# Dividing by the softmax sum after the V product, and chunk outputs inside the recurrence, in a two-layer RWKV-7/MLA decoder trunk

## The chip, the cores and the metric

The kernel runs on one core of a Trainium2 chip, as one program. The metric is the device time of one execution in microseconds (us), median of several runs. All times below are of this chip.

## What is computed

Two layers of a decoder trunk on 512 tokens, D = 1024, in float32, then a final RMSNorm. Each layer has a mixer and a gated MLP with a short convolution. The mixer runs two token mixers side by side on projections of the same normalised input. The reference, cut to the parts that the change touches:

```python
def step(state, inp):                      # RWKV-7, 8 heads x 64, one token after the other
    r_t, w_t, k_t, v_t, a_t, b_t = inp
    sa = einsum('bhij,bhj->bhi', state, a_t)
    state = state * w_t[:, :, None, :] + sa[..., None] * b_t[:, :, None, :] + v_t[..., None] * k_t[:, :, None, :]
    return state, einsum('bhij,bhj->bhi', state, r_t)
...
mu = mean(y, -1); var = mean(square(y - mu), -1)          # a norm per token and head
y = (y - mu) * rsqrt(var + LNX_EPS) * lnx_w + lnx_b
y_a = (y + bonus) * gate @ W_oA
...
s = (q_nope . k_nope + q_rope . k_rope) * scale           # MLA attention, 8 heads, causal, blocks of 128 queries
p = softmax(where(key_pos <= q_pos, s, NEG_INF), axis=-1)
y_b = (p @ v) @ W_oB
...
h = h + (sigmoid(g_A) * y_a + sigmoid(g_B) * y_b) @ W_out
```

## The kernel before

Activations lie transposed: 128 channels on the partitions, 512 tokens along the free axis. Large products are done with three float32r matmuls (a high and a low part of each operand, `mm3`, lines 245 to 248). Weights come as units of eight 128x128 blocks through SyncE's queue (`produce`, line 205); each is cast to its high part by ScalarE (line 201) and its low part is formed by VectorE (line 202), with two buffers each.

A mixer has three stages. The first projects and prepares, for each pair of heads, the matrices of the RWKV-7 recurrence over eight chunks of 64 tokens (`AM`, `AR`, `BT`, values in `Z`). The second inverts the small triangular matrices in `AM` and makes the latent projections of the attention. The third, from line 770, holds the change. It does two things at a time:

- **The recurrence** (loop over `c` from line 910). For each chunk: the product of the state with `AR` (line 918), a sum on VectorE into `xs` (line 921), the product with `AM` (line 928), a copy into `Z` (line 930), the product with `BT` (line 937), and the new state `St` from it and `tmp`, which GpSimd makes (lines 943 and 944). Each step needs the one before it.
- **The attention** (a generator, line 777). First remaining projections, then values `Vt` for all heads, then for each pair of heads p = 0..3 and query block b = 0..3 one step t = 4p + b: `scores(p, b)` (two products into two `sc` banks; VectorE adds the causal mask and takes the row minimum, line 834; ScalarE takes the exponential with its row sum, line 837; VectorE takes the reciprocal of the sum, line 838; ScalarE scales the row, line 839). One step later `turned` transposes each head's block with TensorE into the one `pt` bank (line 846) and copies it out to `PT`, by VectorE where b is even and ScalarE where it is odd (line 848). Two steps later `values` multiplies with `Vt` into the bank `po` (line 857); after b = 3 `split` casts `po` into the operand of the output projection (lines 279 and 280). Between these lie the projections of the next pair of heads (`project`, extra products with `q` on line 818 and `K` on lines 806 and 807), and in the last pair the first products of the RWKV output projection (`ow`).

TensorE's order is as traced (`manual_schedule`). `filler(n)` takes n segments of the attention, from one `yield` to the next, and puts them into TensorE's order between the steps of the recurrence, so that TensorE has work while the other engines prepare the next step. Before the change the recurrence takes 37 segments: up to the end of step t = 3. The order on the other engines, and on SyncE's queue for transfers, is set by a planner when the kernel is built, by its own estimate of when each instruction is ready; an engine then works in that order.

After the recurrence come four `chunk_out` (lines 951 to 971: the outputs of two chunks each, from `AR`, `St`, `AM` and `Z` into the two banks of `xy`, and a copy by ScalarE back to `Z`), with two segments behind each; then the norms of all four (`group_norm`: sums, mean and square on VectorE and ScalarE, the power on GpSimd on line 984; `group_scale` on GpSimd, line 989); six segments; then `yop` for each pair of heads: four transposes of `Z` into a bank of `xy` (line 993), two loads into the two buffers of the tag `yl` (lines 995 and 997), a product-and-sum and a product on VectorE (lines 998 and 999), and a split. Two segments stand after each two `yop`. Then the rest of the attention runs without anything between, and the rest of the RWKV output projection (`wtile(yops)`) follows.

PSUM has eight banks in this stage: two `sc`, two `xy`, one `pt`, one `po`, two for accumulation. `qk` has eight buffers of 128x512, for `K` and `q` of two pairs of heads.

Of the kernel before, what the change touches and what calls it, by code (L numbers as in the profile page):

```python
# [158 lines left out]
def build(ctx, tc, x, pos, wst, vecd, constd, out):  # L159
# [265 lines left out]
    def mixer(l, ops, nrm, wks):  # L425
        with ExitStack() as mx:
# [343 lines left out]
            with pool(name=f"tb{l}", bufs=2) as tb:  # L770
                def MT(name, tag, bufs=3):
                    return tb.tile([128, 512], F32, name=name, tag=tag, bufs=bufs)
# [4 lines left out]
                def attention(yops, ow):  # L777
# [22 lines left out]
                    def project(p):  # L800
                        psk = acc()
                        mm3(psk, [w[:, 128 * p:128 * p + 128] for w in lk], kvop, True, True)
                        ks[p] = []
                        for hh in range(2):
                            K = MT("K", "qk", 8)
                            A.copy(K[0:64, :], psk[64 * hh:64 * hh + 64, :])
                            G.tensor_copy(K[64:128, :], kp[64:128, :])
                            ks[p].append(K)
                        yield
                        qs[p] = []  # L810
                        for hh in range(2):
                            psq = acc()
                            for j in range(2):
                                mm3(psq, W.get(), qops[j], j == 0, j == 1)
                                if j == 0:
                                    yield
                            q = MT("q", "qk", 8)
                            V.tensor_tensor(q, psq, rq, ALU.mult)  # L818
                            qs[p].append(q)
                            yield  # L820

                    Ps, PTs, po = {}, {}, {}

                    def scores(p, b):
                        n = 128 * (b + 1)
                        sps = [sc(), sc()]
                        for hh in range(2):
                            PE.matmul(sps[hh][:, 0:n], qs[p][hh][:, 128 * b:128 * b + 128], ks[p][hh][:, 0:n],  # L828
                                      start=True, stop=True)
                        Ps[p, b] = []  # L830
                        for hh in range(2):
                            P = MT("P", "P", 4)
                            mn = tb.tile([128, 4], F32, name="mn", bufs=6)
                            V.tensor_tensor_reduce(out=P[:, 0:n], in0=sps[hh][:, 0:n],  # L834
                                                   in1=cst[:, C_CAUS + 512 - n:C_CAUS + 512], scale=-ATT_SCALE,
                                                   scalar=1e30, op0=ALU.add, op1=ALU.min, accum_out=mn[:, 0:1])
                            A.activation(P[:, 0:n], P[:, 0:n], AF.Exp, bias=mn[:, 0:1], scale=-1.0, accum_out=mn[:, 1:2])  # L837
                            V.reciprocal(mn[:, 2:3], mn[:, 1:2])  # L838
                            A.activation(P[:, 0:n], P[:, 0:n], AF.Copy, scale=mn[:, 2:3])  # L839
                            Ps[p, b].append(P)  # L840
# [10 lines left out]
                    def values(p, b):  # L851
# [8 lines left out]
                        if b == 3:  # L860
                            oops.append(split(xp, po[p], None, "xb", 8))

                    yield from project(0)
                    steps = [(p, b) for p in range(4) for b in range(4)]
                    for t in range(18):
# [41 lines left out]


                St = [None]
                for c in range(8):  # L910
# [3 lines left out]
                    if c:  # L914
# [34 lines left out]


                def chunk_out(i):
                    xy = xyt()
                    for p in range(4):
                        for e, hh in ((0, 0), (1, 1), (0, 1), (1, 0)):
                            c = 2 * i + e
                            ur, vr = rows(e)
                            k0 = 64 * hh
                            if c:
                                PE.matmul(xy[vr:vr + 64, hh, 64 * p:64 * p + 64], AR[p][k0:k0 + 64, c, vr:vr + 64],
                                          St[c][k0:k0 + 64, p, :], start=p == 0, stop=False, tile_position=(k0, vr))  # L960
                    for hh in range(2):
                        for p in range(4):
                            for e in range(2):
                                c = 2 * i + e
                                ur, vr = rows(e)
                                hd = 2 * p + hh
                                PE.matmul(xy[vr:vr + 64, hh, 64 * p:64 * p + 64], AM[:, hd, c, vr:vr + 64],
                                          Z[:, i, e, 64 * hd:64 * hd + 64], start=c == 0 and p == 0, stop=p == 3,
                                          tile_position=(0, vr))
                    A.copy(Z[:, i, 0, :].rearrange("p (q h i) -> p q h i", h=2, i=64),  # L970
                           xy[:, :, 0:256].rearrange("p h (q i) -> p q h i", i=64))


                def group_norm(i):
                    Y = Z[:, i, 0, :].rearrange("p (h i) -> p h i", i=64)
                    s2 = Z[:, i, 1, :].rearrange("p (h i) -> p h i", i=64)
                    mu = tb.tile([128, 24], F32, name="mu", bufs=4)
                    V.tensor_reduce(mu[:, 0:8], Y, mybir.AxisListType.X, ALU.add)
                    V.tensor_scalar(mu[:, 0:8], mu[:, 0:8], 1.0 / 64, None, ALU.mult)
                    V.tensor_tensor(Y, Y, mu[:, 0:8, None].to_broadcast([128, 8, 64]), ALU.subtract)  # L980
                    A.activation(s2, Y, AF.Square)
                    V.tensor_reduce(mu[:, 8:16], s2, mybir.AxisListType.X, ALU.add)
                    V.tensor_scalar(mu[:, 8:16], mu[:, 8:16], 1.0 / 64, LNX_EPS, ALU.mult, ALU.add)
                    G.tensor_tensor(mu[:, 16:24], mu[:, 8:16], mhalf[:, 0:8], ALU.pow)  # L984
                    return mu[:, 16:24]

                def group_scale(i, gr):
                    Y = Z[:, i, 0, :].rearrange("p (h i) -> p h i", i=64)
                    G.tensor_tensor(Y, Y, gr[:, :, None].to_broadcast([128, 8, 64]), ALU.mult)  # L989

                def yop(ps, p):
# [177 lines left out]
```

## Time and profile before

| what | value |
|---|---|
| three runs | 1609.90, 1610.43, 1611.07 us |
| median | 1610.43 us |
| profiled execution | 1608.68 us |
| its span, from the first instruction to the last | 1606.9 us |
| share of TensorE in the chain of work that ended last | 90% |
| the same of VectorE, ScalarE, GpSimd | 5%, 2%, 2% |
| bytes moved | 166.08 MB, a mean of 103 GB/s |

The profile is of one execution. Its page and the views of its trace use short names: PE is TensorE's matmuls, PEld its weight loads, DVE is VectorE, ACT is ScalarE, POOL is GpSimd, SP is SyncE. L846 is line 846 of the kernel. An entry `out<-in` names the tiles written and read. A line of the view of waits reads "engine, tile, line that waited <- engine, tile, line that ended the wait: us in all, times, the longest". The granted clock is TensorE's: 1.00 is full speed. The chain is followed back from the last instruction, at each step to what released it. In a timeline the columns are start and duration in us, then engine, line, operation and shape, and in brackets the time that the engine stood idle ahead of it and what ended that.

### The profile page before, as it was taken

The page shows a single profiled execution, that of the slowest core. Times are in us where ns is not written, and L with a number is a line of the kernel's source. Part 1 is how long each engine was busy: PE and PEld are TensorE (multiplying, and loading weights), DVE is VectorE, ACT ScalarE, POOL GpSimd, SP SyncE. Part 2 cuts the span into 40 slices and gives each one's busy share as a digit, 9 for nine tenths or more (in the row PEclk, how much of TensorE's full clock was granted, in tenths as well). Part 3 has the DMA queues.
Part 4 walks back from the last instruction along what each step waited for, and adds up shares of the span by engine and source line. Part 5 has one row for each costly group of instructions (what it writes and reads, how often), then busy time and mean ns, then how long its engine had stood idle before and what let it go on. Part 6 is the DMA issues. An engine that isn't in the chain of part 4 may idle for free.

```text
span 1606.9 us, 22378 instructions
## 1 busy us (share of the span) xinstructions
PE 1559.8 (97%) x9052; PEld 1259.2 (78%) x9052; DVE 916.8 (57%) x1468; ACT 661.8 (41%) x996; POOL 188.7 (12%) x156
## 2 busy tenths in 40 slices
PE   8999999889999999999999999997999999999998
PEld 6887886668888888888878888765688888888887
DVE  6578786656555555533346768756465555554333
ACT  6445344563443333322244443455434433333222
POOL 1011002300211101100001111113003111110000
PEclk9999999899999999999999999999999999999999
DMA  6333321224422323233343223212243223233232
GB/s 209 112 102 128 121 85 63 78 63 140 132 92 94 103 92 100 97 105 123 116 136 112 95 97 117 87 61 79 66 152 124 92 92 105 92 95 102 92 101 83
DMA packets 57272, 166.08 MB, mean 103 GB/s; under 512 B 6352, under 2 KB 8528, under 8 KB 57168
## 3 DMA queue, kind: packets, MB, share of 16 engines
q1 hardware_dynamic: 57024, 164.48, 31.2%
q8 instruction: 71, 1.16, 0.3%
q14 instruction: 33, 0.27, 0.1%
q10 hardware_dynamic: 144, 0.16, 0.0%
HBM read 147.32 MB, written 17.30 MB: 102 GB/s over the span
## 4 chain that ended last, share of the span: by engine, by line
PE 90%; DVE 5%; ACT 2%; POOL 2%; issue 1%; DMA 1%; POOLq 0%; DVEq 0%; SPq 0%; ACTq 0%
PE acc L246 26%; PE acc L247 26%; PE acc L248 26%; PE sc L828 2%; PE xy L928 1%; PE pt L846 1%; PE m L599 1%; POOL mu L984 1%; PE po L857 1%; PE m L607 1%; ACT whi L201 1%; POOL Z L989 1%; DVE wlo L202 1%; ACT P L837 1%; ACT P L839 0%
## 5 line engine op out<-in xcount | busy, mean ns | idle before, releaser
L246 PE MATMUL acc<-hi,whi 128*128 128x512 f32 (+1 forms) x1910 | 755.1, 395 | 6.3 <-ACT hi L282 5.2
L248 PE MATMUL acc<-hi,wlo 128*128 128x512 f32 (+1 forms) x1910 | 742.1, 389 | 0.6 <-DVE wlo L202 0.6
L247 PE MATMUL acc<-lo,whi 128*128 128x512 f32 (+1 forms) x1910 | 741.1, 388 | 0.0
L201 ACT CAST whi<-raw 128x1024 fp32r<-128x1024 f32 (+2 forms) x249 | 253.4, 1019 | 546.9 <-PE acc L247 468.6
L246 PEld LDWEIGHTS acc<-hi,whi 128*128 128x128 f32 x1910 | 359.6, 188 | 82.8 <-ACT hi L282 5.2
L248 PEld LDWEIGHTS acc<-hi,wlo 128*128 128x128 f32 x1910 | 359.5, 188 | 75.8 <-DVE wlo L202 1.0
L247 PEld LDWEIGHTS acc<-lo,whi 128*128 128x128 f32 x1910 | 359.8, 188 | 72.3 <-DVE lo L283 0.5
L202 DVE TENSOR_TENSOR wlo<-raw,whi 128x1024 fp32r<-128x1024 f32 (+2 forms) x249 | 308.3, 1240 | 177.8 <-ACT whi L201 177.3
L1089 POOL TENSOR_TENSOR c<-c,rstd 128x512 f32<-128x512 f32 x44 | 58.0, 1317 | 403.5 <-ACT c L1088 403.5
L1082 DVE TENSOR_TENSOR u<-acc,rstd 128x512 f32<-128x512 f32 x44 | 30.4, 692 | 104.7 <-PE acc L248 104.6
L1091 DVE TENSOR_TENSOR c<-c,acc 128x512 f32<-128x512 f32 x44 | 30.3, 688 | 86.4 <-POOL c L1089 86.4
L1088 ACT ACTIVATE c<-c 128x512 f32<-128x512 f32 x44 | 27.8, 632 | 81.6 <-DVE c L1087 81.6
L837 ACT ACTIVATE P<-P,mn 128x128 f32<-128x128 f32 (+3 forms) x64 | 35.7, 558 | 57.4 <-DVE mn L834 57.0
L341 POOL TENSOR_TENSOR nacc<-nacc,nsq 128x512 f32<-128x512 f32 x14 | 25.1, 1790 | 245.4 <-ACT nsq L340 245.4
L305 POOL TENSOR_TENSOR nv<-nv,cst 128x4 f32<-128x4 f32 (+1 forms) x10 | 10.0, 996 | 352.1 <-DVE nv L304 352.1
L828 PE MATMUL sc<-K,q 128*128 128x128 f32 (+3 forms) x128 | 47.2, 494 | 1.3 <-DVE q L818 1.3
L834 DVE CUSTOM_DVE_ANT_0 P<-sc,cst 128x128 f32<-128x128 f32 (+3 forms) x64 | 30.5, 488 | 30.2 <-PE sc L828 29.5
L846 PE MATMUL pt<-cst,P 128*128 128x128 f32 x160 | 32.0, 301 | 15.5 <-ACT PT L848 11.5
L450 DVE TENSOR_TENSOR cur<-acc,rstd 128x512 f32<-128x512 f32 x28 | 19.1, 689 | 46.9 <-PE acc L248 39.3
L846 PEld LDWEIGHTS pt<-cst,P 128*128 128x128 f32 x160 | 20.6, 151 | 28.4 <-ACT PT L848 14.5
L1085 ACT ACTIVATE c<-u,vec 128x512 f32<-128x512 f32 x44 | 35.7, 811 | 2.8 <-DVE u L1081 2.8
L839 ACT ACTIVATE P<-P,mn 128x128 f32<-128x128 f32 (+3 forms) x64 | 33.2, 553 | 5.6 <-DVE mn L838 5.4
(242 smaller groups left out, 1374.9 us busy)
## 6 DMA issues: line engine op xcount, KB each, us to landing
raw<-in_w SPq DMA_DIRECT2D x238, 512.0 KB, 3.4
gate_d<-gg SPq DMA_DIRECT2D x32, 256.0 KB, 2.1
AM<-gate_d SPq DMA_DIRECT2D x16, 256.0 KB, 4.3
gb<-gate_d SPq DMA_DIRECT2D x16, 256.0 KB, 3.7
h<-in_x SPq DMA_DIRECT2D x8, 256.0 KB, 4.1
rgate_d<-gt SPq DMA_DIRECT2D x8, 256.0 KB, 2.7
bl_d<-rk SPq DMA_DIRECT2D x8, 256.0 KB, 2.0
bl<-bl_d SPq DMA_DIRECT2D x8, 256.0 KB, 2.6
```

The source lines that it names most:

```text
L201: A.copy(hi, r)
L202: V.tensor_tensor(lo, r, hi.bitcast(F32), ALU.subtract)
L246: PE.matmul(ps, w[0], xx[0], start=first, stop=False)
L247: PE.matmul(ps, w[0], xx[1], start=False, stop=False)
L248: PE.matmul(ps, w[1], xx[0], start=False, stop=last)
L828: PE.matmul(sps[hh][:, 0:n], qs[p][hh][:, 128 * b:128 * b + 128], ks[p][hh][:, 0:n], start=True, stop=True)
L834: V.tensor_tensor_reduce(out=P[:, 0:n], in0=sps[hh][:, 0:n], in1=cst[:, C_CAUS + 512 - n:C_CAUS + 512], scale=-ATT_SCALE, scalar=1e30, op0 ...
L837: A.activation(P[:, 0:n], P[:, 0:n], AF.Exp, bias=mn[:, 0:1], scale=-1.0, accum_out=mn[:, 1:2])
L839: A.activation(P[:, 0:n], P[:, 0:n], AF.Copy, scale=mn[:, 2:3])
L846: PE.transpose(pt[:, 128 * kb:128 * kb + 128], Ps[p, b][hh][:, 128 * kb:128 * kb + 128], ident)
L1085: A.activation(cc, u[:, 2:514], AF.Identity, bias=vc(l, "conv_b", i), scale=vc(l, "conv_w", 2 * FT + i))
L1089: G.tensor_tensor(cc, cc, rstd, ALU.mult)
```

## The change

Five things change together.

1. The exponentials of the attention are no longer scaled. The row sums of a pair of heads go into columns of one small tile `sums[p]`, and reciprocals and scalings per block go away. One step after the last block of a pair (`inverse`, t = 4p + 4) VectorE takes the eight reciprocals at once and GpSimd spreads them into a 128x512 tile `r`. At the end of the next step (`inverse_rows`, t = 4p + 5) TensorE transposes `r` in four blocks into the `pt` bank. The last values product of the pair (`values(p, 3)`) is put behind these transposes, where it was between the two `turned` of that step. Then ScalarE copies `po` to `o`, VectorE multiplies `o` with the `pt` bank, and `o` is split as `po` was.
2. `chunk_out` for the first three pairs of chunks moves into the recurrence, at c = 2, 4 and 6, in place of two segments each, and each is followed at once by its norm and scaling. It writes to two `sc` banks in place of `xy`, and ScalarE copies it out in two halves.
3. The recurrence thus takes 31 segments. After it come `chunk_out(3)`, its norm, and ten segments in place of six and of the two behind each `chunk_out`. `yop` is as it was.
4. `qk` has seven buffers in place of eight; there is a new tag `R` with two.
5. The size of the scratch for dynamic DMA is 512 in place of 1024.

The diff without the unchanged bodies of `group_norm` and `group_scale`, which only move up:

```diff
-                            K = MT("K", "qk", 8)
+                            K = MT("K", "qk", 7)
...
-                            q = MT("q", "qk", 8)
+                            q = MT("q", "qk", 7)
...
+                        if b == 0:
+                            sums[p] = tb.tile([128, 16], F32, name="ls", bufs=2)
                         for hh in range(2):
                             P = MT("P", "P", 4)
-                            mn = tb.tile([128, 4], F32, name="mn", bufs=6)
+                            mn = tb.tile([128, 1], F32, name="mn", bufs=6)
+                            j = 2 * b + hh
...
-                            A.activation(P[:, 0:n], P[:, 0:n], AF.Exp, bias=mn[:, 0:1], scale=-1.0, accum_out=mn[:, 1:2])
-                            V.reciprocal(mn[:, 2:3], mn[:, 1:2])
-                            A.activation(P[:, 0:n], P[:, 0:n], AF.Copy, scale=mn[:, 2:3])
+                            A.activation(P[:, 0:n], P[:, 0:n], AF.Exp, bias=mn[:, 0:1], scale=-1.0,
+                                         accum_out=sums[p][:, j:j + 1])
...
                         if b == 3:
-                            oops.append(split(xp, po[p], None, "xb", 8))
+                            o = MT("o", "R", 2)
+                            A.copy(o, po[p])
+                            V.tensor_tensor(o, o, inv[p], ALU.mult)
+                            oops.append(split(xp, o, None, "xb", 8))
+
+                    inv = {}
+
+                    def inverse(p):
+
+                        V.reciprocal(sums[p][:, 8:16], sums[p][:, 0:8])
+                        r = MT("r", "R", 2)
+                        G.tensor_copy(r.rearrange("p (j i) -> p j i", i=64), sums[p][:, 8:16, None].to_broadcast([128, 8, 64]))
+                        return r
+
+                    def inverse_rows(p, r):
+                        inv[p] = pb.tile([128, 512], F32, name="pt", tag="pt")
+                        for b in range(4):
+                            PE.transpose(inv[p][:, 128 * b:128 * b + 128], r[:, 128 * b:128 * b + 128], ident)
...
                             turned(*steps[t - 1], 0)
-                        if t > 1:
+                        if t > 1 and t % 4 != 1:
                             values(*steps[t - 2])
+                        elif t > 4:
+                            late = steps[t - 2]
                         if 0 < t < 17:
                             yield
                             turned(*steps[t - 1], 1)
+                        if t and t % 4 == 0:
+                            r = inverse(t // 4 - 1)
+                        if t > 1 and t % 4 == 1:
+                            inverse_rows(t // 4 - 1, r)
+                            values(*late)
                         yield
...
+                def chunk_out(i):
+                    ps = [sc("co"), sc("co")]
+                    begun = set()
+
+                    def put(e, hh, p, w, x, pos, last):
+                        ur, vr = rows(e)
+                        PE.matmul(ps[hh][vr:vr + 64, 64 * p:64 * p + 64], w, x, start=(e, hh) not in begun, stop=last,
+                                  tile_position=(pos, vr))
+                        begun.add((e, hh))
...
+                    for hh in range(2):
+                        A.copy(Z[:, i, 0, :].rearrange("p (q h i) -> p q h i", h=2, i=64)[:, :, hh, :],
+                               ps[hh][:, 0:256].rearrange("p (q i) -> p q i", i=64))
...
                         xs = xs.rearrange("p q h i -> p (q h) i")
-                        filler(2)
+                        if c in (2, 4, 6):
+                            chunk_out(c // 2 - 1)
+                            gr = group_norm(c // 2 - 1)
+                            group_scale(c // 2 - 1, gr)
+                        else:
+                            filler(2)
...
-                for i in range(4):
-                    chunk_out(i)
-                    filler(2)
-                grs = []
-                for i in range(4):
-                    grs.append(group_norm(i))
-                for i, gr in enumerate(grs):
-                    group_scale(i, gr)
-                filler(6)
+                chunk_out(3)
+                group_scale(3, group_norm(3))
+                filler(10)
...
-    nc = _bacc.Bacc("TRN2", target_bir_lowering=False, num_devices=1, dynamic_dma_scratch_size=1024)
+    nc = _bacc.Bacc("TRN2", target_bir_lowering=False, num_devices=1, dynamic_dma_scratch_size=512)
```

More of the change, by code (lines that the diff above doesn't have):

```diff
@@ L820, in project @@
                             yield
-                    Ps, PTs, po = {}, {}, {}
+                    Ps, PTs, po, sums = {}, {}, {}, {}
                     def scores(p, b):
@@ L906, in filler @@
                         next(att, None)
+                def chunk_out(i):
[6 more added lines that the diff above has]
+                        begun.add((e, hh))
+                    for p in range(4):
+                        for e, hh in ((0, 0), (1, 1), (0, 1), (1, 0)):
+                            c, k0 = 2 * i + e, 64 * hh
+                            vr = rows(e)[1]
+                            if c:
+                                put(e, hh, p, AR[p][k0:k0 + 64, c, vr:vr + 64], St[c][k0:k0 + 64, p, :], k0, False)
+                    for hh in range(2):
+                        for p in range(4):
+                            for e in range(2):
+                                vr = rows(e)[1]
+                                hd = 2 * p + hh
+                                put(e, hh, p, AM[:, hd, 2 * i + e, vr:vr + 64], Z[:, i, e, 64 * hd:64 * hd + 64], 0,
+                                    p == 3)
+                    for hh in range(2):
+                        A.copy(Z[:, i, 0, :].rearrange("p (q h i) -> p q h i", h=2, i=64)[:, :, hh, :],
+                               ps[hh][:, 0:256].rearrange("p (q i) -> p q i", i=64))
@@ new lines, in group_norm @@
+                def group_norm(i):
+                    Y = Z[:, i, 0, :].rearrange("p (h i) -> p h i", i=64)
+                    s2 = Z[:, i, 1, :].rearrange("p (h i) -> p h i", i=64)
+                    mu = tb.tile([128, 24], F32, name="mu", bufs=4)
+                    V.tensor_reduce(mu[:, 0:8], Y, mybir.AxisListType.X, ALU.add)
+                    V.tensor_scalar(mu[:, 0:8], mu[:, 0:8], 1.0 / 64, None, ALU.mult)
+                    V.tensor_tensor(Y, Y, mu[:, 0:8, None].to_broadcast([128, 8, 64]), ALU.subtract)
+                    A.activation(s2, Y, AF.Square)
+                    V.tensor_reduce(mu[:, 8:16], s2, mybir.AxisListType.X, ALU.add)
+                    V.tensor_scalar(mu[:, 8:16], mu[:, 8:16], 1.0 / 64, LNX_EPS, ALU.mult, ALU.add)
+                    G.tensor_tensor(mu[:, 16:24], mu[:, 8:16], mhalf[:, 0:8], ALU.pow)
+                    return mu[:, 16:24]
@@ L909, in mixer, with group_scale @@
+                def group_scale(i, gr):
+                    Y = Z[:, i, 0, :].rearrange("p (h i) -> p h i", i=64)
+                    G.tensor_tensor(Y, Y, gr[:, :, None].to_broadcast([128, 8, 64]), ALU.mult)
                 St = [None]
@@ L948, in mixer @@
                         filler(1)
[L951 to L971, printed above, removed]
@@ L974, in group_norm @@
[L974 to L985, printed above, removed]
@@ L987, in group_scale @@
-                def group_scale(i, gr):
-                    Y = Z[:, i, 0, :].rearrange("p (h i) -> p h i", i=64)
-                    G.tensor_tensor(Y, Y, gr[:, :, None].to_broadcast([128, 8, 64]), ALU.mult)
                 def yop(ps, p):
```

## The prediction

> **What bounds the kernel now.** I read the page first, for the share of each engine, then the table of stretches for the stage that the change touches, then the waits of TensorE in that stage, and the chain and the timelines only at the places that these waits name. In the page the first number of an engine is its busy time, the percentage its share of the span:
>
> ```profile
> PE 1559.8 (97%) x9052; PEld 1259.2 (78%) x9052; DVE 916.8 (57%) x1468; ACT 661.8 (41%) x996; POOL 188.7 (12%) x156
> ```
>
> TensorE is the bound, and its order is written out by hand. An instruction less on another engine is worth nothing unless TensorE waits for it. The change lies in the last stage of the mixer, once in each layer. The two rows give start and end, length, then the busy time of PE, PEld, DVE, ACT and POOL, the granted clock, and the DMA share:
>
> ```profile
> 232.00:365.00 133.00, 118.30 (x1120) 85.60 (x1115) 77.26 (x197) 69.65 (x155) 23.26 (x23) 0.94 0.23 73
> 1025.00:1160.00 135.00, 118.63 (x1153) 86.36 (x1154) 78.97 (x198) 69.99 (x156) 23.16 (x23) 0.96 0.23 73
> ```
>
> In 133 us TensorE stands idle for 14.7, in the second 135 for 16.4, and for some of the rest its clock is down. ACT and DVE are half idle: neither is a second bound. Who makes TensorE wait is in the view of waits, first layer 0, then layer 1 (total, times, longest):
>
> ```profile
> PE pt L846 <- ACT PT L848: 5.4, 3, 3.3
> PE xy L993 <- DVE bl L998: 4.7, 2, 3.8
> PE xy L993 <- POOL Z L989: 1.9, 1, 1.9
> PE pt L846 <- DVE PT L848: 1.7, 3, 0.9
> PE sc L828 <- DVE q L818: 0.7, 1, 0.7
> ```
>
> ```profile
> PE pt L846 <- ACT PT L848: 6.1, 4, 3.3
> PE xy L993 <- DVE bl L998: 4.7, 2, 3.8
> PE pt L846 <- DVE PT L848: 2.0, 4, 0.9
> PE xy L993 <- POOL Z L989: 1.9, 1, 1.9
> PE sc L828 <- DVE q L818: 0.7, 1, 0.7
> PE xy L993 <- DVE mn L838: 0.6, 1, 0.6
> ```
>
> That is 14.4 and 16.0 us. Each of the longest two waits is followed by a slow spell. The rows are two 4 us stretches of layer 0, one behind the wait of 3.8 and one behind that of 3.3, with a clock of 0.50; below them the chain shows the same scores (four records of 128x512) in a slow and in a full-speed place:
>
> ```profile
> 316.00:320.00 4.00, 4.00 (x15) 3.57 (x15) 1.73 (x8) 1.88 (x7) 0.00 (x0) 0.50 0.00 0
> 332.00:336.00 4.00, 3.74 (x6) 1.73 (x7) 1.10 (x3) 1.15 (x3) 0.00 (x0) 0.50 0.42 135
> ```
>
> ```profile
> 332.95 3.41 PE sc L828 x4
> ...
> 350.53 1.72 PE sc L828 x4
> ```
>
> So the question is which of these waits the change takes away, and which it makes. All terms below are per layer.
>
> **What it takes off other engines.** 32 normalisations on ACT and 32 reciprocals on DVE go; four copies, four products and four broadcast copies come. This is off the path, hidden under TensorE's work, except where a normalisation stands ahead of a copy that TensorE waits for. There is one such place, the wait of 3.3 at step t = 10. ACT's queue there:
>
> ```profile
> 328.17 1.05 ACT L201 CAST whi<-raw 128x1024 fp32r<-128x1024 f32 x1 [1.18 <-PE acc L247]
> ...
> 330.33 0.60 ACT L279 CAST hi<-bl 128x512 fp32r<-128x512 f32 x1
> 330.84 1.11 ACT L839 ACTIVATE P<-P,mn 128x384 f32<-128x384 f32 x2
> 331.86 0.35 ACT L848 COPY PT<-pt 128x256 f32<-128x256 f32 x1
> ```
>
> The copy of PT comes last, behind the cast of a weight unit, two exponentials, a cast of yop and two normalisations. Without these two it starts 1.0 earlier, 1.5 if the cast of yop has also moved away: I take 1.3 off and leave 2.0. The other two waits for ACT share 2.1; at t = 14 nothing but exponentials is left ahead of the copy, so I take 1.0 off there, and let 1.1 stand at t = 2. With a wait of 2.0 instead of 3.3 I take the slow spell behind it as gone: 1.7 from the scores (3.41 against 1.72) and 0.4 from the matmuls behind them, 2.1. If the clock falls all the same, that comes back.
>
> [...]
>
> **What it adds to TensorE.** The chain has four transposes of 128x128, one transpose alone, and a values call of four blocks:
>
> ```profile
> 341.62 0.59 PE pt L846 x4
> ...
> 344.47 0.11 PE pt L846
> 344.58 1.05 PE po L857 x16
> ```
>
> Sixteen transposes of r are 4 x 0.59 = 2.4, and nothing hides them: they are TensorE's own time.
>
> **The order around pt.** At t = 4p+5 the order was turned(0), values (1.05), turned(1); now it is turned(0), turned(1), four transposes into pt, then values. There is one pt bank. The values call was the cover of the copy out of it; now TensorE waits for that copy twice in a row. This is the copy on DVE:
>
> ```profile
> 272.88 0.29 DVE L848 COPY PT<-pt 128x128 f32<-128x128 f32 x1 [0.42 <-PE pt L846]
> ```
>
> A wait is at least about that 0.3; the longest wait for DVE above is 0.9, where another DVE pass stood ahead. I take 0.55, nearer to the bare copy, because DVE is half idle. Pairs 0 to 2 have two waits each (t = 17 has no turned): 6 x 0.55 = 3.3, between 1.8 and 5.4.
>
> Then pt is held on, until o is copied out of po and multiplied by the broadcast in pt. The nearest rows are today's two passes over po:
>
> ```profile
> L279 ACT CAST hi<-po x4: 561/586/586, 298.8 to 362.9; 128x512 fp32r<-128x512 f32 x4
> L280 DVE TENSOR_TENSOR lo<-po,hi x4: 680/686/691, 300.2 to 363.5; 128x512 fp32r<-128x512 f32 x4
> ```
>
> 0.59 and 0.69 with the hand-overs are some 1.5. The cover is the scores of the next step and one projection product:
>
> ```profile
> 326.37 1.29 PE sc L828 x4
> 327.66 0.24 PE acc L246
> ```
>
> 1.29 + 3 x 0.24 = 2.0. That holds if ACT and DVE take the two at once. ACT then also has the exponentials of these scores ahead of the next copy of PT. I take 1.2 at t = 6 (p = 1, no such wait today), 0.5 more at t = 10 and 0.3 at t = 14: 2.0, between 0 and two waits of 3.3. The last pair costs nothing further: its two casts are due only after 17 projection products of 0.7 each, 12 us.
>
> **chunk_out and the norms.** The recurrence gives up 6 of its 37 segments and takes three chunk_outs, which are the same matmuls at another time. They cover the pass over xs as the segments did. Their norms put DVE passes in front of the copy of Z that TensorE needs next; the nearest row is the 0.69 above, one pass at each of three places at the worst, 2.1, nothing at best. I take 0.4, since segments follow. On POOL the product for tmp could fall behind a norm's power; tmp is due only a chunk later, so nothing. chunk_out(3) now wants both sc banks straight after scores(0,2) filled them: up to two DVE passes, 1.4; I take one, 0.7. The wait of 1.9 for POOL goes, because ten segments stand between the last norm and yop. The wait for q (0.7) and those for DVE's PT (1.7) go, since other work now stands between; the new ones are counted above.
>
> The yop waits stay. Three L998 on DVE:
>
> ```profile
> 305.31 0.75 DVE L998 SCALAR_TENSOR_TENSOR bl<-xy,vec,bl 128x512 f32<-128x512 f32 x1 [2.12 <-PE xy L993]
> ...
> 310.16 0.75 DVE L998 SCALAR_TENSOR_TENSOR bl<-xy,vec,bl 128x512 f32<-128x512 f32 x1
> ...
> 314.70 0.75 DVE L998 SCALAR_TENSOR_TENSOR bl<-xy,vec,bl 128x512 f32<-128x512 f32 x1 [2.60 <-DMA bl<-bl_d]
> ```
>
> They stand 4.9 and 4.5 apart, the pace at which the two slots of tag yl are freed and loaded again, and the change leaves that code alone. Inside these 9.4 us TensorE had scores(1,3), one turned and one values; now, ten segments earlier in the attention, it has one turned and scores(1,1). By the rows above (1.72 and about 1.0, against 0.59 and about 0.9) that is 1.2 less work under the same wait; I take 1.0, as DVE is freer. The slow spell behind it stays.
>
> **Sum.** Added: 2.4 + 3.3 + 2.0 + 0.4 + 0.7 + 1.0 = 9.8. Taken away: 1.3 + 1.0 + 2.1 + 1.9 + 0.7 + 1.7 = 8.7. Layer 0 loses 1.1. In layer 1 the waits for DVE are 0.3 more and that for mn, 0.6, goes too: it loses 0.2. Together +1.3. The profiled execution took 1608.7 (span 1606.9), so 1610.0 against it; the median of the runs is 1.7 above it, so 1611.7 there. No change: about 3.2 us, 0.2%, is what a measurement of this kernel can tell from none.
>
> **Rivals.** *Faster: the copy of PT goes ahead of the exponentials.* The planner orders ACT, and at t = 6 it did just that:
>
> ```profile
> 301.88 0.37 ACT L848 COPY PT<-pt 128x256 f32<-128x256 f32 x1 [1.10 <-PE pt L846]
> 302.14 0.62 ACT L837 ACTIVATE P<-P,mn 128x384 f32<-128x384 f32 x1
> ```
>
> With less on ACT it may do so at every step. Then what I left standing goes: 1.1 at t = 2, 1.2 at t = 6, 2.0 at t = 10, 4.3 per layer, 8.6 in all: 1603. Against it: the queue at t = 10 above. Chance 0.33.
>
> *Slower: pt is released late.* The copy of o sits on ACT behind a cast and exponentials as the copy of PT did, and TensorE stands before the single pt bank. It decides as soon as the copy starts more than 0.5 us late, what the 2.0 of cover leaves over the 1.5. One wait of 3.3 per layer in place of 0.6, with its slow spell of 2.1, is 4.8, or 9.6 in all: 1621. For it: two engines now stand between values and the release. Against: DVE and ACT are half idle. Chance 0.20.
>
> *Slower: the clock stays down.* Behind yop now come single transposes, waits, and then four more transposes instead of projections. If such work does not bring the clock back, the transposes (0.6), values (1.05) and scores (1.29) of t = 5 run at half speed as well: 3.0 per layer, 6 in all: 1618. [...] Against: the projections ahead of them at t = 5. Chance 0.11. [...]
>
> **How the numbers follow.** The forecast, that gains and losses cancel, has 0.36, with a range of its own from 1607 to 1615: 0.31 of it lies within 0.2% and 0.05 above. Faster is the first rival, 0.33; slower is 0.20 + 0.11 + 0.05 = 0.36; the same 0.31. The range from 1601 to 1621 leaves out the lower end of the first rival and the upper end of the second, about 0.1 each.
>
> **What would show it.** Right: the two L998 gaps near 4.5 again, with longer idle before the second pair of yop; no wait of L993 for POOL; two short waits of pt for DVE at each t = 4p+5; the wait at t = 10 down to about 2 and clock 1.00 behind it; TensorE's idle in each stage near 14 to 17. Wrong: a wait of 3 us or more at pt that ends with the product of o (late release), a stage with under 10 us idle (the waits behind ACT went), or waits inside the recurrence, where I have put nearly nothing.

## The result and the profile after

The changed kernel took 1617.97 us, median of five runs (1616.05 to 1618.83), against 1610.00 for the kernel before (1606.26 to 1611.07). The ratio is 1.0052, with a 95% interval from 1.0037 to 1.0067: slower by half a per cent. That lies inside the whole range (1601 to 1621), but above the range of the forecast itself (1607 to 1615), by which gains and losses cancel (+1.3).

The profiled execution took 1617.96 us, its span 1616.1, 9.2 more than before. The busy line of its page (the lines of the changed kernel have other numbers: the transposes of the probabilities are L848 and their copy L850, before L846 and L848; values is L859; the transposes in yop are L1029 and its product-and-sum L1034, before L993 and L998; L864, L865 and L880 are the copy of `o`, its product and the transposes of `r`):

```profile
PE 1561.4 (97%) x9084; PEld 1261.1 (78%) x9084; DVE 914.7 (57%) x1420; ACT 637.3 (39%) x948; POOL 192.5 (12%) x164
```

ACT lost 24.5 us of work and 48 instructions, and the kernel became slower: ACT was not the bound. TensorE has the 32 added transposes, 16 per layer. To compare the stages fairly, the next two tables have one row per layer, cut at the same two instructions in both kernels, from the second group of L760 to the first sums of the MLP. The columns are start and end, length, the busy time of PE, PEld, DVE, ACT and POOL, the granted clock, the DMA share and GB/s. First before, then after:

```profile
231.43:449.37 217.94, 203.24 (x1513) 155.00 (x1513) 127.64 (x257) 100.21 (x195) 35.79 (x30) 0.96 0.30 96
1024.99:1242.57 217.58, 201.21 (x1513) 153.72 (x1513) 127.56 (x257) 100.02 (x195) 35.68 (x30) 0.98 0.30 96
```

```profile
232.98:453.31 220.33, 201.48 (x1529) 154.29 (x1529) 126.56 (x233) 87.95 (x171) 37.63 (x34) 0.98 0.30 95
1028.96:1252.15 223.19, 203.87 (x1529) 155.82 (x1529) 126.73 (x233) 88.02 (x171) 37.67 (x34) 0.96 0.29 94
```

Length less busy time is TensorE's idle time: 14.7 and 16.4 before, 18.8 and 19.3 after. Layer 0 is 2.4 longer: 4.1 more idle and 1.8 less busy, although 16 transposes came, because less of the work ran at a low clock (the granted clock of the row is 0.98 against 0.96). Layer 1 is 5.6 longer: 2.9 more idle (0.8 of it at the stage's first instructions, where nothing in the profile ends it) and 2.7 more busy. Of the 9.2 of the span, 8.0 are made in the stage; 1.55 arise ahead of it in layer 0, in code that the change does not touch.

The view of waits for layer 0 after (layer 1 has the same lines, 7.1, 4.5, 3.5 and 2.0 for the first four):

```profile
PE xy L1029 <- DVE bl L1034: 7.3, 3, 4.2
PE pt L848 <- ACT PT L850: 4.6, 4, 2.3
PE pt L848 <- DVE PT L850: 3.5, 5, 1.2
PE pt L880 <- DVE PT L850: 2.0, 3, 1.0
PE xy L990 <- DVE St L1021: 0.8, 1, 0.8
PE co L941 <- DVE mn L837: 0.3, 1, 0.3
```

The waits for POOL and for q are gone. Those of yop are up from 4.7 to 7.3, and those for DVE's copy of PT from 1.7 to 3.5 + 2.0. No wait ends with the product of `o`.

How this looks at one pair of heads (steps t = 9 and 10, layer 0, TensorE's timeline):

```profile
326.72 0.27 PE L848 MATMUL pt<-cst,P 128*128 128x128 f32 x1
327.38 0.33 PE L848 MATMUL pt<-cst,P 128*128 128x128 f32 x1 [0.38 <-DVE PT L850]
328.76 0.63 PE L880 MATMUL pt<-cst,r 128*128 128x128 f32 x4 [1.05 <-DVE PT L850]
329.31 1.09 PE L859 MATMUL po<-PT,Vt 128*64 128x128 f32 x16
...
335.48 0.44 PE L848 MATMUL pt<-cst,P 128*128 128x128 f32 x2 [2.30 <-ACT PT L850]
335.75 2.67 PE L828 MATMUL sc<-K,q 128*128 128x512 f32 x4
```

TensorE fills the one `pt` bank and stands, fills it and stands again; only then comes the values product, which it could have done in the first of these gaps. ACT's queue ahead of the wait of 2.30:

```profile
330.46 0.58 ACT L864 COPY o<-po 128x512 f32<-128x512 f32 x1 [2.77 <-PE po L859]
331.80 0.62 ACT L279 CAST hi<-o 128x512 fp32r<-128x512 f32 x1 [0.75 <-DVE o L865]
332.40 1.04 ACT L201 CAST whi<-raw 128x1024 fp32r<-128x1024 f32 x1
...
335.08 0.34 ACT L850 COPY PT<-pt 128x256 f32<-128x256 f32 x1
```

ACT is idle for 2.77 until values is through, then for 0.75 until DVE has multiplied `o`; the casts of `o`, of a weight unit and of `bl` and two exponentials follow, and the copy of PT that TensorE needs stands behind all of them. Which of them made the wait is in the chain:

```profile
332.13 0.25 PE acc L247
...
332.40 0.49 ACT whi L201
...
```

The weight cast was released by TensorE's own projection (until 332.38), at the moment at which the cast of `o` ended, so the cast of `o` did not delay it. The late values product thus costs at t = 9, where it no longer covers the copies. That it also delays the copy of PT at t = 10 is not shown by this chain: a weight cast stood ahead of that copy before the change as well.

In layer 1 the clock stayed down behind yop until the scores of t = 6; in layer 0 it was back at 310 us (0.50 from 304 to 308 us, 0.65 from 308 to 310, 1.00 from 310 to 315), ahead of the transposes of `r`. Two stretches of 5 us of layer 1, then TensorE's timeline there:

```profile
1100.00:1105.00 5.00, 2.81 (x9) 2.43 (x10) 1.13 (x2) 0.00 (x0) 0.00 (x0) 0.50 0.12 43
1105.00:1110.00 5.00, 4.14 (x25) 2.83 (x23) 0.90 (x3) 0.00 (x0) 0.00 (x0) 0.50 0.00 0
```

```profile
1107.41 1.09 PE L880 MATMUL pt<-cst,r 128*128 128x128 f32 x4 [0.47 <-DVE PT L850]
1108.43 1.98 PE L859 MATMUL po<-PT,Vt 128*64 128x128 f32 x16
```

The four transposes take 1.09 and values 1.98; at full clock, at t = 9 above (1.00 from 328 to 331 us), they take 0.63 and 1.09.

### The profile page after: what moved, and what is told of

Read it like the earlier page. It is cut to its first block, busy times and chain, and to the rows that moved or that the text cites. A ratio compares the mean times of both kernels' runs of the same rounds, so it can differ in the third digit from the quotient of the medians.

```text
span 1616.1 us, 22429 instructions
## 1 busy us (share of the span) xinstructions
PE 1561.4 (97%) x9084; PEld 1261.1 (78%) x9084; DVE 914.7 (57%) x1420; ACT 637.3 (39%) x948; POOL 192.5 (12%) x164
## 4 chain that ended last, share of the span: by engine, by line
PE 90%; DVE 6%; ACT 2%; issue 1%; DMA 1%; POOL 0%; DVEq 0%; POOLq 0%; SPq 0%; ACTq 0%
PE acc L246 26%; PE acc L247 26%; PE acc L248 26%; PE sc L828 1%; PE xy L1005 1%; PE pt L848 1%; PE m L599 1%; PE po L859 1%; PE co L941 1%; ACT P L840 1%; DVE wlo L202 1%; PE m L607 1%; PE m L583 0%; DVE P L837 0%; PE xy L1014 0%
## 5 line engine op out<-in xcount | busy, mean ns | idle before, releaser
L840 ACT ACTIVATE P<-P,mn 128x128 f32<-128x128 f32 (+3 forms) x64 | 35.6, 557 | 46.9 <-DVE mn L837 44.8
L848 PE MATMUL pt<-cst,P 128*128 128x128 f32 x160 | 30.7, 291 | 16.6 <-ACT PT L850 9.1
L848 PEld LDWEIGHTS pt<-cst,P 128*128 128x128 f32 x160 | 19.9, 145 | 31.8 <-ACT PT L850 12.5
L828 PE MATMUL sc<-K,q 128*128 128x128 f32 (+3 forms) x128 | 43.1, 460 | 0.0
L1117 DVE SCALAR_TENSOR_TENSOR c<-u,vec,c 128x512 f32<-128x512 f32 x44 | 33.1, 752 | 1.5
```

Source lines behind the costliest of these rows:

```text
L848: PE.transpose(pt[:, 128 * kb:128 * kb + 128], Ps[p, b][hh][:, 128 * kb:128 * kb + 128], ident)
L1117: V.scalar_tensor_tensor(cc, u[:, 0:512], vc(l, "conv_w", i), cc, ALU.mult, ALU.add)
```

## The experiments

The theory after the comparison: not the division costs the time, but its place, between the two `turned` and `values`. Its rivals: the chunk outputs and norms inside the recurrence cost it; or the division's own work does, the transposes and the product; or the clock that yop leaves down does. All ratios are against the kernel before, run beside the experiment.

### Which half

**e1** is the kernel before with parts 1, 4 and 5 of the change; against the changed kernel:

```diff
-                        if c in (2, 4, 6):
-                            chunk_out(c // 2 - 1)
-                            gr = group_norm(c // 2 - 1)
-                            group_scale(c // 2 - 1, gr)
-                        else:
-                            filler(2)
+                        filler(2)
...
-                chunk_out(3)
-                group_scale(3, group_norm(3))
-                filler(10)
+                for i in range(4):
+                    chunk_out(i)
+                    filler(2)
...
+                filler(6)
```

> Only the division behind the V product (with its scratch size and seven buffers for K and q); chunk outputs and norms as before. Theory one, the loss lies in the division: 16 transposes (2.2 us per layer in the trace of the changed kernel) and the waits of t = 5, 9, 13 for the one pt bank (3.6) cost 5.8 per layer, the shorter waits at t = 10 and 14 give back 2 to 3: 1616 to 1618 us against 1610 before. Theory two, the loss lies in the moved chunk outputs: 1609 to 1612.

**e2** is the other half, the kernel before with parts 2 and 3; against the changed kernel:

```diff
-                            A.activation(P[:, 0:n], P[:, 0:n], AF.Exp, bias=mn[:, 0:1], scale=-1.0,
-                                         accum_out=sums[p][:, j:j + 1])
+                            A.activation(P[:, 0:n], P[:, 0:n], AF.Exp, bias=mn[:, 0:1], scale=-1.0, accum_out=mn[:, 1:2])
+                            V.reciprocal(mn[:, 2:3], mn[:, 1:2])
+                            A.activation(P[:, 0:n], P[:, 0:n], AF.Copy, scale=mn[:, 2:3])
...
-                        if t > 1 and t % 4 == 1:
-                            inverse_rows(t // 4 - 1, r)
-                            values(*late)
```

> Only the chunk outputs and norms inside the recurrence; division and buffers as before. Theory one: 1608 to 1612, because what the wait for GpSimd (1.9 per layer) and the covered waits give is taken back by longer waits before yop. Theory two: 1615 to 1618.

Measured: e1 1614.41 us, ratio 1.0036 (1.0023 to 1.0050); e2 1605.72, 0.9977 (0.9966 to 0.9987). The division loses 5.6 us, the chunk outputs gain 3.1. The waits of e1 in layer 0, then those of e2:

```profile
PE xy L1019 <- DVE bl L1024: 6.1, 3, 4.3
PE pt L848 <- DVE PT L850: 3.5, 5, 1.2
PE pt L848 <- ACT PT L850: 2.7, 2, 2.3
PE pt L880 <- DVE PT L850: 1.7, 3, 0.6
...
```

```profile
PE pt L846 <- ACT PT L848: 7.1, 5, 3.3
PE xy L1003 <- DVE bl L1008: 4.9, 2, 4.0
PE xy L1003 <- DVE mn L838: 2.3, 1, 2.3
...
```

e1 has the new waits for DVE at `pt`, with nearly the figures of the changed kernel (3.5 and 1.7 against 3.5 and 2.0), so they come from the division. e2 has none of them, keeps the wait of 3.3 at t = 10, has one for `mn` (2.3) in place of that for POOL, and is faster all the same. So the norms in the recurrence are not the loss. Both times lie outside what was expected of them, e1 between its two theories and e2 below both. And the halves do not add up: 5.6 - 3.1 = 2.5, against 8.0 for both.

### What in the division

**e4** leaves out the reciprocals, `r`, its transposes and the product, so that its output lacks the division by the softmax sum; `values` stays behind both `turned`.

```diff
-                            V.tensor_tensor(o, o, inv[p], ALU.mult)
...
-                        if t and t % 4 == 0:
-                            r = inverse(t // 4 - 1)
                         if t > 1 and t % 4 == 1:
-                            inverse_rows(t // 4 - 1, r)
                             values(*late)
```

> The changed kernel with the division left out: no reciprocals, no r, no transposes of it, no product; the output lacks the softmax sum. The last values product stays behind both turned. Theory one: 2.2 of transposes and about 2 of waits per layer go, and the product no longer holds pt: 1607 to 1611. Theory two: only the transposes' own time goes, 1613 to 1615.

**e8** keeps the division where the change has it, but puts `values` back between the two `turned`; ACT's copy of `po` goes with it, the product stays with the transposes (`divided` is as printed under e3).

```diff
-                        if t > 1 and t % 4 != 1:
+                        if t > 1:
                             values(*steps[t - 2])
-                        elif t > 4:
-                            late = steps[t - 2]
...
                         if t > 1 and t % 4 == 1:
-                            inverse_rows(t // 4 - 1, r)
-                            values(*late)
+                            divided(t // 4 - 1, r)
```

> The changed kernel with only the last values product put back between the two turned; the transposes of r still come straight behind the second turned. One wait of each pair (0.4, 0.4, 0.9 at t = 5, 9, 13) goes, the other stays. If the waits alone are the loss: about 1614 to 1616 (1618 changed, 1601 with both moved). If the loss is that everything behind values, the copy of o and its cast, comes late on ACT and makes the wait at t = 10 and its slow clock: 1604 to 1608.

**e3** also moves the transposes of `r`, the product and the split behind the scores of the next step (t = 4p + 6; for the last pair they stay at t = 17):

```diff
+                    def divided(p, r):
+                        inverse_rows(p, r)
+                        V.tensor_tensor(os[p], os[p], inv[p], ALU.mult)
+                        oops.append(split(xp, os[p], None, "xb", 8))
...
                             scores(p, b)
+                            if t > 5 and t % 4 == 2:
+                                divided(t // 4 - 1, r)
...
-                        if t > 1 and t % 4 == 1:
-                            inverse_rows(t // 4 - 1, r)
-                            values(*late)
+                        if t == 17:
+                            divided(3, r)
```

> The changed kernel, but the last values product of a pair stands between the two turned again, and the transposes of r and the product with them come one step later, behind the scores of t = 4p+6 and ahead of the projection there. Same work, other order around pt. Theory one: of the 3.6 per layer at t = 5, 9, 13 some 3 go: 1611 to 1613. If the transposes' own time is the loss and not the order, or the loss lies in the chunk outputs: 1616 to 1618.

**e6** is e1 with e3's order, the covered division without the chunk part. Against the kernel before, beside part 1:

```diff
                             scores(p, b)
+                            if t > 5 and t % 4 == 2:
+                                divided(t // 4 - 1, r)
...
+                        if t and t % 4 == 0:
+                            r = inverse(t // 4 - 1)
+                        if t == 17:
+                            divided(3, r)
```

> Only the division behind V in the order of e3_cover, chunk outputs and norms as before. Theory one (order around pt): the 5.6 us that e1_softmax lost turn into a gain like that between the changed kernel and e3_cover (17), so 1597 to 1603. If the cover works only together with the moved chunk outputs: 1607 to 1612.

| kernel | us | ratio (95%) | against the changed kernel's median |
|---|---|---|---|
| e4 | 1602.35 | 0.9960 (0.9948 to 0.9971) | -15.6 |
| e8 | 1608.86 | 0.9997 (0.9985 to 1.0008) | -9.1 |
| e3 | 1600.73 | 0.9949 (0.9937 to 0.9961) | -17.2 |
| e6 | 1605.06 | 0.9970 (0.9958 to 0.9982) | -12.9 |

The last column compares medians that were measured at different times; the kernel before took 1608.85 to 1610.00 beside them, so it is good to about 1 us. e3 does the whole division, with the same instructions as the changed kernel, and is no slower than e4, which does none. So the same work costs 17 us less in another order on TensorE, with what the planner makes of it on the other engines: the order is the loss. Parts 4 and 5 of the change are in e3 and e6 too, which are faster than the kernel before, so they are not the loss either. e3 and e4 came out far below what was expected (by 10 and 5 us), e8 about 1 us above the second of its two ranges; the expectation for e3 had priced the waits alone. The waits of e3 in layer 0, then TensorE and ACT at the pair shown above:

```profile
PE xy L1033 <- DVE bl L1038: 7.2, 3, 4.1
PE pt L848 <- DVE PT L850: 2.6, 3, 1.2
PE pt L848 <- ACT PT L850: 1.8, 3, 1.0
...
PE pt L848 <- DVE o L870: 0.5, 2, 0.4
```

```profile
325.02 0.27 PE L848 MATMUL pt<-cst,P 128*128 128x128 f32 x1
325.23 1.09 PE L859 MATMUL po<-PT,Vt 128*64 128x128 f32 x16
326.25 0.33 PE L848 MATMUL pt<-cst,P 128*128 128x128 f32 x1
326.42 1.46 PE L828 MATMUL sc<-K,q 128*128 128x384 f32 x4
327.71 0.60 PE L885 MATMUL pt<-cst,r 128*128 128x128 f32 x4
```

```profile
326.37 0.58 ACT L864 COPY o<-po 128x512 f32<-128x512 f32 x1 [0.38 <-PE po L859]
...
329.56 0.60 ACT L279 CAST hi<-o 128x512 fp32r<-128x512 f32 x1
330.07 0.36 ACT L850 COPY PT<-pt 128x256 f32<-128x256 f32 x1
...
331.28 1.05 ACT L201 CAST whi<-raw 128x1024 fp32r<-128x1024 f32 x1
```

Between the fillings of `pt` now stands a product each time, and none of these lines of TensorE has an idle bracket; the two fillings of t = 10 behind them wait 0.38 and 0.29. On ACT the copy of `o` comes early, and the planner has put the weight cast behind the copies of PT.

Of the 17.2 us between the changed kernel and e3, e8 has 9.1, by the cover of `values` and what the planner makes of it on ACT. This is no share that stands by itself: e4 leaves `values` late and still gains 15.6, so the late product alone, without the transposes of `r` behind it, does not keep the loss. At t = 10 of e8, TensorE and then ACT:

```profile
331.04 0.44 PE L848 MATMUL pt<-cst,P 128*128 128x128 f32 x2 [0.98 <-ACT PT L850]
331.32 1.88 PE L828 MATMUL sc<-K,q 128*128 128x512 f32 x4
```

```profile
330.62 0.36 ACT L850 COPY PT<-pt 128x256 f32<-128x256 f32 x1
330.89 1.05 ACT L201 CAST whi<-raw 128x1024 fp32r<-128x1024 f32 x1
```

The wait is 0.98 and the clock up (1.00 from 330 to 340 us, against 0.84 in the changed kernel): 1.3 less wait and 0.8 less for the scores, 2.1 in this place. The weight cast, which made the wait of 2.30, now stands behind the first copy of PT. The other 8.1 go when the transposes, the product and the split move behind the scores. e6 was expected between 1597 and 1603 and missed that by 2. It does agree with two other pairs: the covered division is worth 4.3 us without the chunk part (e6 against its kernel before), 5.0 with it (e3 against e2), and 4.5 between e5 and e9 below. Placed as in the change it costs 5.6 alone (e1), but 12.2 beside the chunk part (changed kernel against e2), and 11.1 between e10 and e9 below. Why twice as much is not settled.

### The clock behind yop

The longest single wait in all kernels so far is yop's, 3.8 to 4.3 in layer 0 (4.7 to 7.5 in all). DVE waits there for the load of `bl` (2.8 us in layer 0 before, the longest 2.6, and 3.3 in the changed kernel); I take the two buffers of `yl`, which neither half touches, as the cause, but no run varies their number. **e7** is the kernel before with yop spread out, one pair of heads at a time:

```diff
-                for p in range(0, 4, 2):
-                    ps = xyt()
-                    yop(ps[:, 0, :], p)
-                    yop(ps[:, 1, :], p + 1)
-                    filler(2)
+                for p in range(4):
+                    yop(xyt()[:, 0, :], p)
+                    filler(4)
```

> The kernel before with yop spread as in e5_cover_yop, nothing else. The waits of yop for L998 there are 4.7 us per layer, longest 3.8, each followed by slow clock. If they are a separate loss that neither half of the change touches: 1597 to 1603 against 1609 before. If not: 1606 to 1610.

**e5** is e3, **e10** the changed kernel and **e9** e2, each with this same edit.

> The kernel of e3_cover with each yop by itself in xy and four attention segments behind each, in place of two yops in a row with two segments behind the pair. If the waits of yop (7.2 us per layer in e3_cover) and the slow clock behind them are only a matter of what stands beside them, most of both goes: 6 us of waits and about 2 of slow clock per layer, 1585 to 1589 us against 1601 for e3_cover. If segments taken there are missing later and the waits for ACT and DVE come back in the last steps: 1595 to 1601.

> The changed kernel with yop spread, order around pt as in the change. If the loss of the order around pt is independent of the yop waits: 18 us above e5_cover_yop as the changed kernel is 17 above e3_cover, so 1599 to 1602. If a good part of it was the slow clock that yop hands on to t = 5 (the clock is 0.50 there in layer 1 of the changed kernel until the values product): 1590 to 1596.

> Only the chunk outputs inside the recurrence and yop spread; the softmax rows are scaled by ScalarE as before, no transposes of r. Against e5_cover_yop (1583) it tells whether the division behind V, well covered, is worth anything. If it is worth its transposes (4.4 us in all) because the queue of ScalarE is shorter: e9 is slower, 1586 to 1591. If scaling on ScalarE was hidden all along and the transposes are a plain loss: e9 is faster, 1578 to 1581.

| kernel | us | ratio (95%) |
|---|---|---|
| e7, before + yop spread | 1589.63 | 0.9878 (0.9864 to 0.9892) |
| e9, chunk part + yop spread | 1587.37 | 0.9865 (0.9849 to 0.9881) |
| e10, changed + yop spread | 1598.51 | 0.9942 (0.9922 to 0.9962) |
| e5, e3 + yop spread | 1582.86 | 0.9838 (0.9822 to 0.9854) |

The spread is worth 17.9 to 19.7 us wherever it is put (1617.97 to 1598.51, 1600.73 to 1582.86, and 19.7 for e7). e10 stays 15.6 above e5, as the changed kernel was 17.2 above e3. The change costs 8.9 with the spread (e10 against e7) and 8.0 without. So the loss of the order at `pt` is there with and without the waits of yop and the slow clock behind them (in layer 1 of e10 the granted clock is 1.00 in each stretch of 10 us from 1070 to 1120 us): that rival falls as the cause, and is a second, larger loss beside it. e7 and e5 came out 7 and 2 below what was expected, e10 half a us below the first of its ranges; e9 and, below, e11 lie inside one of theirs. e5 is the fastest kernel of the study and beats both. Its waits in layer 0:

```profile
PE pt L848 <- ACT PT L850: 2.0, 4, 1.0
PE pt L848 <- DVE PT L850: 1.9, 2, 1.2
...
```

No line of yop is left. **e11** is e5 with the copies of PT shared out otherwise:

```diff
-                        (A.copy if b % 2 else V.tensor_copy)(PT[:, 0:n], pt[:, 0:n])
+                        (A.copy if hh else V.tensor_copy)(PT[:, 0:n], pt[:, 0:n])
```

> e5_cover_yop with the two copies of PT of a step on two engines, the first on VectorE and the second on ScalarE, in place of both on one. The waits left in e5_cover_yop are about 4 us per layer for PT, two of them behind a full queue of VectorE (1.2 at t = 3, 0.7 at t = 7) and 1.0 behind ScalarE at t = 8. If two short queues are better than one: 1578 to 1581. If each copy then finds the longer queue: 1583 to 1588.

1584.83 us, ratio 0.9850 (0.9836 to 0.9864), no gain over e5 (intervals overlap): its waits for ACT went, and those for DVE rose to 4.1, the longest 1.9. Here another engine for the copy only changed whose queue it stood in.

How much of each difference is idle time, and how much the clock? The sums of both layers, in the profiled executions, with the stage cut as in the tables above. Kernels with the transposes of `r` have 32 x 0.14 = 4.5 us of work more than those without.

| kernel | idle, us | busy, us |
|---|---|---|
| before | 31.07 | 404.45 |
| changed | 38.17 | 405.35 |
| e1 | 31.72 | 412.23 |
| e2 | 34.63 | 396.81 |
| e8 | 33.46 | 398.63 |
| e3 | 27.80 | 397.88 |
| e6 | 24.94 | 404.66 |
| e10 | 25.25 | 398.77 |
| e5 | 13.56 | 397.96 |

The covered order takes idle time away in each pair of kernels with the same instructions: 10.4 (changed kernel and e3), 11.7 (e10 and e5), 6.8 (e1 and e6). Of busy time it takes 7.5, 0.8 and 7.6. There the instructions are the same, so I read this as the clock (in layer 0, in stretches of 10 us from 300 to 340 us, the granted clock is 0.83, 0.82, 0.84 and 0.85 in e1, and 0.83, 0.83, 1.00 and 1.00 in e6); it does not come every time. e8 gains 4.7 of idle and 6.7 of busy time: by this reading, more clock than waits. e1 stands idle about as long as the kernel before, because its new waits for DVE come in place of waits for ACT and POOL; its loss is 7.8 of busy time, 4.5 of it the transposes, and the rest I read as the clock. And e2 is faster with 3.6 more idle time, because it is busy 7.6 less.

## Why the prediction was right and wrong

**Right.** The waits for POOL and q went. The 16 transposes take 4 x 0.56 = 2.2 in layer 0 (2.4 foretold), and the six waits at `pt` of t = 5, 9 and 13 sum to 0.39 + 0.47 + 0.38 + 1.05 + 0.87 + 0.47 = 3.6 (3.3). The recurrence and the score banks cost 0.8 + 0.3 (0.4 + 0.7). ACT's waits came out at 4.6 (5.4 - 1.3 - 1.0 + 2.0 = 5.1), but 0.96 of it stood at t = 8, where none was foretold, and none at t = 14, so the sum is right in part by luck. The first rival did not come: the planner kept the copy of PT behind exponentials. Nor did the second, the late release of `pt`: nothing waits for the product of `o`.

**Wrong, the idle time of the stage.** I foretold 14 to 17 us and found 18.8 and 19.3. Two terms of the sum are at fault:

- "The wait for q (0.7) and those for DVE's PT (1.7) go, since other work now stands between". For the second there was no row. They came back at other places, 1.17 at t = 3 and 0.70 at t = 7: 1.9 per layer. Why there is not shown.
- "I take 1.0, as DVE is freer" for yop. The waits rose by 2.6. The pace of the two slots is nearly unchanged: the three product-and-sums of yop on DVE start 9.0 us apart from first to last, 9.4 before. So the work that is taken out of these gaps comes back as idle. The prediction had priced this work at full clock, the scores at 1.72. They had run slower there before, as the first line shows; the other two are of the changed kernel, where the scores between the yops take 1.03 at 297.21:

```profile
306.60 2.90 PE L828 MATMUL sc<-K,q 128*128 128x512 f32 x4
```

```profile
300.46 0.63 PE L1029 MATMUL xy<-cst,Z 128*128 128x128 f32 x4 [2.22 <-DVE bl L1034]
305.34 1.12 PE L1029 MATMUL xy<-cst,Z 128*128 128x128 f32 x4 [4.25 <-DVE bl L1034]
```

**Wrong, the slow spell at t = 10.** I took a wait of 2.0 and its spell as gone (2.1); that a wait cut to 2.0 spares the clock was my estimate. But my own sum left 2.0 + 0.5 there, and 2.30 was measured; the scores behind it still took 2.50 in the chain against 3.41 before and 1.72 at full clock (1.00 from 350 to 360 us before). So 0.9 was saved of 1.7 in the scores. Layer 0 was helped elsewhere: before, the clock was low in two stretches full of work, between the yops (0.66 from 308 to 312 us, 3.66 busy, with the slow scores above) and behind them (0.50 from 316 to 320 us, 4.00 busy); now it was low where much was idle (0.50 from 304 to 308 us, 2.66 busy). So it ended only 1.3 above the forecast for it.

**Wrong, layer 1.** The third rival, "the clock stays down", held there and not in layer 0. It was priced at 3.0 per layer; transposes, values and scores took 1.09, 1.98 and 2.14 there against 0.63, 1.09 and 1.56 in layer 0, which is 1.9. That the total of 1618 for this rival meets the median is luck, since it counted both layers. The granted clock of layer 1 was 0.50 from 1100 to 1110 us, until projections, transposes and values had passed, and 0.85 from 1110 to 1115. Layer 0, with the same order, had 1.00 from 310 to 336 us. So the order alone does not decide this place, and what does is not shown.

**Right in part, the order around pt.** I saw that the cover of the copies went and priced the waits at t = 5, 9 and 13 rightly. The wait at t = 10 also came out near its sum (2.30 against 2.5). What I did not see is the clock behind it, and that the place of the weight cast in ACT's queue, which the planner sets, goes with this wait: ahead of the copy of PT it was 2.30, behind it 0.98 (e8) and 0.29 (e3).

**Open.** Why the division as placed costs twice as much with the chunk part as alone, and how much of it is chance in the clock. By the table of idle and busy time it adds 3.5 of idle time beside the chunk part and 0.7 alone, but 8.5 and 7.8 of busy time, which is nearly the same. The intervals of the ratios are some 2 to 3 us to either side, and single executions of one kernel spread by up to 10 (e10: 1594.41 to 1604.32). The profiled executions of e1, e4 and e5 were the slowest of their runs (e1: 1618.29 against a median of 1614.41), so the waits are read from them and the times from the medians, and the busy times of e1 and e5 in the table may be too high. What sets the clock in each place stays open.

## What to carry to other kernels

Where one PSUM bank is filled, copied out and filled again, write down the TensorE work that stands between two fillings before moving any of it: the same division cost 5.6 us without that work and gained 4 to 5 with it. An edit of TensorE's order can also change the order that the planner gives the other engines, so the queue of the engine that frees the bank has to be written out anew. And look first for the longest wait in the stage: spreading the two-buffer loads of yop was worth 18 to 20 us, more than all five parts of the change.

## What the runs showed that was not expected

The same wait does not always bring the clock down. e10 has the same wait of 2.30 at t = 10 as the changed kernel, and its scores behind it run in 1.88 where those of the changed kernel take 2.67:

```profile
325.57 0.44 PE L848 MATMUL pt<-cst,P 128*128 128x128 f32 x2 [2.30 <-ACT PT L850]
325.85 1.88 PE L828 MATMUL sc<-K,q 128*128 128x512 f32 x4
```

And a slow spell can come with no idle time at all. The stretch from 204 to 208 us, ahead of the stage and in identical code, before and then after:

```profile
204.00:208.00 4.00, 4.00 (x23) 3.45 (x22) 3.19 (x10) 1.55 (x3) 1.63 (x2) 1.00 0.39 133
```

```profile
204.00:208.00 4.00, 4.00 (x15) 3.18 (x13) 2.50 (x7) 1.53 (x3) 1.16 (x1) 0.62 0.44 133
```

TensorE is busy for all 4.00 us in both, with 23 matmuls at a clock of 1.00 and 15 at 0.62, and in the 8 us ahead of them too (from 200 to 204 us the granted clock was 1.00 before and 0.95 after). By an estimate from the clock, 4.00 x (1 - 0.62) = 1.5, this is most of the 1.55 us by which the stage of the changed kernel began later, and the stage began anywhere from 231.15 us (e7) to 235.71 us (e5) in the profiled executions. Differences of a few us between single executions prove nothing here.
